# A two-layer S5 and linear-attention trunk: the first layer opens with all four u tiles accumulated together over k

## Chip, cores and metric

The kernel runs on 1 core of one Trainium2 chip. The metric is the time of one execution on the device in microseconds, as the median of several runs. A profile of one further execution is used to read where the time goes. TensorE is PE in the rows, VectorE DVE, ScalarE ACT, GpSimd POOL, and SP is the engine that issues the transfers.

## What is computed

The input x is 512 tokens of 1024 features. Each of two layers does this (cut from the reference, in float32):

```python
h = rmsnorm(x, norm_mix[i]);  z = h @ w_in[i]            # 1024 x 2064
u, q, k, v, g, gate_lr = split(z)                        # 512, 256, 256, 512, 512, 16 columns
y = s5(u)      # per channel group: complex diagonal recurrence of 64 states, y = Re(C s) + D u
y = gelu(y);  y = y * sigmoid(y @ w_glu + b_glu);  y_s5 = rmsnorm(y, s5_out_norm)
log_a = log_sigmoid(gate_lr @ w_gate + b_gate) / 16      # forget gate of the linear attention
cum = cumsum(log_a in chunks of 64);  q*exp(cum), k*exp(-cum), k*exp(last - cum)
o = causal(q k^T) v + q state;  y_gla = silu(g) * rmsnorm_per_head(o)
x = x + concat(y_s5, y_gla) @ w_out[i]
x = x + swiglu(rmsnorm(x, norm_ffn[i]))                  # 1024 -> 2 x 2816 -> 1024
```

A last RMS norm follows. The S5 part needs tables that depend on parameters alone: the step factor `a` of the recurrence, its powers `a1` to `a4`, the scaled input matrix `bb`, and rotation tables (cosine and sine per state and position).

## The kernel before

**Layout.** Activations are held transposed, features on the 128 partitions and 512 tokens along the free axis, as 8 tiles `xT[k]`. A weight block is 128x128, a weight unit 8 blocks (512 KB), in the order of the list that `block_order` returns. Every weight unit and every activation is split into a rounded half `hi` and a rest `lo`; a product is three matmuls (lines 576 to 578), so a dense tile of 8 k blocks has 24 of them. For a unit, ScalarE converts `hi` (L163) and VectorE subtracts for `lo` (L165). `Weights.ensure` keeps the splits `LOOK` units ahead; raw weights have 2 buffers and split ones 3, so a unit's load waits until the unit two before it is split.

**The RMS norm** is not applied to x. Its factor `rstd` is a row over tokens that scales the products afterwards: `R["rstd"]`. It comes from squares (ScalarE L598), their sum on POOL (L602), a matmul with ones and a logarithm and exponential on ScalarE (`norm`).

**The opening of a layer** is `u_pair`: u tiles 0 and 1 are accumulated together over k, then the 16 matmuls of the gate's low-rank input (`r_tile`, L756), then u tile 2, and inside it, after block k = 3, `stats`: the norm, the scaled row `rsb` (L706), the factor `rU` laid out in S5 order (four copies, L687) and u tile 0's evacuation. `u_copy` has ScalarE copy a u tile from PSUM in 16 pieces of 32x128 into S5 order (L745); `u_scale` then has VectorE multiply it by `rU`, from SBUF into SBUF (L738). `gate_a` does the gate product (L768, needs `rsb`), three passes on ScalarE (L772, L775, L776) and one on VectorE (L774); `gate_c` a subtraction, the cumulative sum and a subtraction on VectorE (L783 to L786); `gate_b` three exponentials (L795 to L797).

**Tables of layer 0** are made beside this in steps, which `bg0` deals out: `prep_small` (small VectorE operations, L304 and its neighbours: first the step, then `a1`, `fr` and `fi`, last `a2` to `a4`), `prep_w` (`bb` on VectorE, the sets with `a2` and `a3` on POOL, `a1` on VectorE, transposes L441 and transfers into `Wk`), `prep_v` (four sets on POOL) and `prep_rot` (rotation tables, on POOL L567 to L572). In layer 0 step 0 of `bg0` stands in `stats`, after `rU`, and makes `a2` to `a4` and `bb`.

**Order.** PE, ScalarE and SP run in the written order throughout; VectorE only in a region of layer 0 that begins at `u_pair` and ends ahead of `v_tiles`, and in the first FFN. Elsewhere VectorE's order, and POOL's everywhere, is set by a scheduler that plans with estimated times.

**Layer 0 after u:** q, k, q, k, then g 0 to 2, then `v_tiles`, whose 8 k steps have hooks for the S5 blocks b = 0 to 3: `s5_fwd` (8 matmuls, four VectorE multiplies L841 to L844 with the rotation tables, two POOL additions L846 and L847, eight scans L852), `s5_back` (four multiplies, POOL L869 and L874), `s5_y` (12 matmuls, 16 pieces of gelu on ScalarE, L899). `score` masks with L982. The GLU follows and needs all four y tiles.

Of the kernel before, what the change touches and what calls it, by code (L numbers as in the profile page):

```python
# [88 lines left out]

def block_order():  # L90
    order = [("in", k, n * P) for k in range(KD) for n in range(2)]
    for n in (2, 3):
        order += [("in", k, n * P) for k in range(KD)]
    for n in (0, 2, 1, 3):
        order += [("in", k, O_Q + n * P) for k in range(KD)]
    for n in range(3):
        order += [("in", k, O_G + n * P) for k in range(KD)]
    for k in range(KD):
        order += [("in", k, O_V + n * P) for n in range(4)]
    order += [("in", k, O_G + 3 * P) for k in range(KD)]  # L100
# [21 lines left out]
ORDER = block_order()  # L122
BIDX = {b: i for i, b in enumerate(ORDER)}
NUNIT = len(ORDER) // UB
assert NUNIT * UB == len(ORDER) == len(BIDX)


class Weights:
# [45 lines left out]
    def get(self, l, blk, width=1):  # L174
        b = BIDX[blk]
# [9 lines left out]
def tile_trunk(  # L185
# [49 lines left out]
    def startup():  # L235
# [411 lines left out]
    def mix(l, xp, nxt, bg):  # L647
# [33 lines left out]

        def unit_rows():
            rU = R["rU"] = act(f"rU{l}", F32, (P, P))
            rv = ntc(R["rstd"])
            for t in range(TS):
                h = slice(32 * t, 32 * t + 32)
                nc.vector.tensor_copy(rU[h].rearrange("p (n c) -> p n c", n=NCH), rv[h, :, t, :])  # L687

        U = {}
# [8 lines left out]
        def u_pair():  # L698
            ps = pair(lambda k: ("in", k, 0), lambda k: ("in", k, P), f"u{l}")
            r_tile()  # L700
            ssq = split(f"sqm{l}", xp.ss.acc) if l else xp.ss.acc

            def stats():
                norm(ssq)
                with tc.high_priority():
                    nc.vector.tensor_tensor(R["r"], R["psr"], R["rstd"], op=M)  # L706
                unit_rows()
                if l == 0:
                    bg()
                u_evac(0, ps[0])  # L710
                W.LOOK = 2

            if l == 0:
                W.LOOK = 1
# [7 lines left out]
            u_evac(2, ps2)  # L722

        def u_tile(b, mid=None):
            ps = dense(lambda k: ("in", k, b * P), f"u{l}{b}")
            if mid is not None:
                mid()
            u_copy(b, ps)
            if l == 0:
                bg()  # L730
            u_scale(b)

        def u_evac(b, ps):
            u_copy(b, ps)
            u_scale(b)

        def u_scale(b):
            nc.vector.tensor_tensor(U[b], U[b], bcast(R["rU"], [P, 4, P], 1), op=M)  # L738

        def u_copy(b, ps):  # L740
            u = act(f"U{l}{b}", F32, (P, 4, P))
            pv = ntc(ps)
# [6 lines left out]
            U[b] = u  # L749

        def r_tile():
            psr = R["psr"] = psum(f"r{l}")
            for k0 in (0, 4):
                for j in range(4):
                    k = k0 + j
                    nc.tensor.matmul(  # L756
                        psr[32 * j:32 * j + 32], wr_s[:, k], xT[k], start=(k0 == 0), stop=(k0 == 4),
                    )
# [278 lines left out]
        hg = cp.tile([P, 8], F32, tag="hg", name=f"hg{l}")  # L1037
        nc.vector.tensor_scalar(hbias, S(l, "bglu"), 0.5, None, op0=M)
        nc.vector.tensor_scalar(hg[:, 0:4], S(l, "s5n"), 0.5, None, op0=M)
        nsilu = 3 if l == 0 else 0  # L1040
        if nsilu:
            nc.vector.tensor_copy(hg[:, 4:4 + nsilu], S(l, "glan")[:, 0:nsilu])
        nc.vector.tensor_scalar(hg[:, 4 + nsilu:8], S(l, "glan")[:, nsilu:], 0.5, None, op0=M)
        ss = SumSq(f"s5{l}")
# [93 lines left out]
        else:  # L1138
            region.enter_context(tc.manual_schedule(engines={mybir.EngineType.DVE}))
            u_pair()  # L1140
            bg()
            bg()
            u_tile(3, lambda: (gate_b(0), gate_b(1)))
            q_tile(0)
            bg()
            k_tile(0)
            bg()
            q_tile(1)
            bg()
            k_tile(1)  # L1150
            bg()
            g_tile(0)
            bg()
# [5 lines left out]
            bg()  # L1159
            region.close()  # L1160
            v_tiles({
# [181 lines left out]
    with tc.manual_schedule(engines={mybir.EngineType.PE, mybir.EngineType.Activation, mybir.EngineType.SP}):  # L1343
        startup()
        xp = XPrep(0, "nmix")
# [6 lines left out]
        next(head)  # L1352
        for k in range(KD):
            xp.split(k)
            if k == 1:
                next(head)
            if k == 3:
                W.LOOK = 1
                W.ensure(0)
            if k > 2:  # L1360
                xp.ss.add(xT[k - 3])
        W.LOOK = 2
        next(small_)
        r_weights(0)
        W.ensure(0)
        for k in range(KD - 3, KD):
            xp.ss.add(xT[k])
        pl = prep_load(0, blks)
        nc.sync.dma_start(cst, const[:, 0:NCST])
        next(small_)  # L1370
        next(rots)
        nc.sync.dma_start(sml[1], small[1])
        pw_ = prep_w(0, nc.vector, pl)
        pv_ = prep_v(0, nc.gpsimd, pl)
        next(pv_)
        step0 = [0]
# [57 lines left out]
def lay_out(a):  # L1434
# [6 lines left out]
    for l in range(DEPTH):  # L1441
        for i, (m, k, c) in enumerate(ORDER):
            wst[l, i // UB, :, i % UB] = f[mats[m]][l, k * P:(k + 1) * P, c:c + P]
# [66 lines left out]
```

## Time and profile before

| | |
|---|---|
| median of 3 runs | 1159.95 us (1159.47 to 1160.25) |
| the profiled execution | 1159.86 us, its span 1158.1 us |
| TensorE busy | 1110.1 us, 96% of the span |
| VectorE busy | 706.2 us, 61% |
| ScalarE busy | 485.6 us, 42% |
| POOL busy | 331.9 us, 29% |
| HBM read | 100.52 MB |

The span is the stretch from the first to the last instruction of the profile. Busy time is summed over the whole span, and stages in it have different limits; the stretches say more. Matmul ends are modelled, and spans on POOL are rough. A group's name says what is written and read; Ln is line n of the kernel before.

### The profile page before, as it was taken

To read this page: it belongs to the slowest core of one execution; us is meant where nothing else is said; L and a number is where in the kernel's file an instruction comes from. 1 tells how busy PE (TensorE), PEld (TensorE's weight loads), DVE (VectorE), ACT (ScalarE), POOL (GpSimd) and SP (SyncE) were. 2 spreads that over 40 slices of the span, in tenths; PEclk is the share of its full clock that TensorE was granted. 3 is DMA by queue.
4 is the path that set the end of the run, shared out by engine and by line. 5 is a ranking of instruction groups with operands and counts; after the bars stand their busy time and mean duration, and the time that the engine had idled before them with its cause. 6 is when DMAs were issued, how large, how long until landed. Compare 5 with 4: busy or idle time off the path is not lost.

```text
span 1158.1 us, 13973 instructions
## 1 busy us (share of the span) xinstructions
PE 1110.1 (96%) x5316; PEld 913.9 (79%) x5316; DVE 706.2 (61%) x947; ACT 485.6 (42%) x844; POOL 331.9 (29%) x322
## 2 busy tenths in 40 slices
PE   8789779999999999999999799999999999999997
PEld 5568658888888888888887688888888888888886
DVE  7996976866454454564466994686545444444454
ACT  6853458443232232432358653745323222222243
POOL 6899544546000052065030440352000000000003
PEclk9899889999999999999999999999999999999999
DMA  6155111244343523232331212123332333223221
GB/s 211 55 112 126 37 37 37 92 130 116 103 109 100 137 91 101 82 109 91 93 104 41 73 61 85 56 91 94 107 100 85 106 99 102 91 91 109 91 91 73
DMA packets 64099, 107.72 MB, mean 93 GB/s; under 512 B 37408, under 2 KB 38304, under 8 KB 64032
## 3 DMA queue, kind: packets, MB, share of 16 engines
q1 hardware_dynamic: 63888, 106.56, 30.2%
q8 instruction: 42, 0.69, 0.2%
q10 hardware_dynamic: 144, 0.26, 0.1%
q14 instruction: 25, 0.20, 0.1%
HBM read 100.52 MB, written 2.10 MB: 89 GB/s over the span
## 4 chain that ended last, share of the span: by engine, by line
PE 79%; DVE 12%; ACT 3%; issue 2%; POOL 2%; DMA 1%; SPq 1%; DVEq 0%; POOLq 0%; ACTq 0%
PE fg L576 7%; PE fg L577 7%; PE fg L578 7%; PE fu L578 7%; PE fu L576 7%; PE fu L577 7%; PE fo L578 7%; PE fo L576 7%; PE fo L577 7%; DVE ro L852 2%; DVE wlo L165 2%; ACT U L745 1%; DVE qz L814 1%; DMA wrr<-in_wr_dram 1%; DMA raw<-in_wst_dram 1%
## 5 line engine op out<-in xcount | busy, mean ns | idle before, releaser
L165 DVE TENSOR_TENSOR wlo<-raw,whi 128x1024 fp32r<-128x1024 f32 x182 | 242.2, 1333 | 113.2 <-ACT whi L163 112.0
L163 ACT CAST whi<-raw 128x1024 fp32r<-128x1024 f32 x183 | 191.8, 1050 | 280.0 <-PE fo L577 116.9
L602 POOL TENSOR_TENSOR sq_fin<-sq_fin 128x512 f32<-128x512 f32 x5 | 6.5, 1296 | 341.8 <-ACT sq_fin L598 341.8
L1237 DVE TENSOR_TENSOR fu<-fu,rs_ffn 128x512 f32<-128x512 f32 x44 | 30.4, 691 | 116.7 <-PE fu L578 113.9
L1254 DVE TENSOR_TENSOR xall<-xall,fo 128x512 f32<-128x512 f32 x78 | 53.1, 686 | 61.9 <-PE fo L578 61.7
L1234 DVE TENSOR_TENSOR fg<-fg,rs_ffn 128x512 f32<-128x512 f32 x44 | 30.3, 688 | 34.7 <-PE fg L578 30.8
L1236 ACT ACTIVATE fg<-fg 128x512 f32<-128x512 f32 x44 | 27.7, 629 | 42.5 <-DVE fg L1234 42.4
L899 ACT ACTIVATE y<-y 32x128 f32<-32x128 f32 x128 | 34.4, 269 | 20.9 <-PE y L890 17.3
L1238 DVE TENSOR_TENSOR fu<-fg,fu 128x512 f32<-128x512 f32 x44 | 31.3, 711 | 5.7 <-ACT fg L1236 1.3
L745 ACT COPY U<-u 32x128 f32<-32x128 f32 x128 | 32.9, 257 | 1.5
L852 DVE TENSOR_TENSOR_SCAN ro<-sp_mag,ro 128x128 f32<-128x128 f32 x64 | 28.5, 507 | 6.6 <-POOL ro L846 6.6
L1089 POOL TENSOR_TENSOR xall<-xall,wo 128x512 f32<-128x512 f32 x16 | 25.5, 1613 | 24.0 <-DVE wo L1088 24.0
L407 POOL TENSOR_TENSOR pt<-bc,sp_a1r 128x256 f32<-128x256 f32 x2 | 1.7, 852 | 94.0 <-issue 92.0
L568 POOL TENSOR_TENSOR rt<-rg 128x512 f32<-128x512 f32 x8 | 10.2, 1288 | 59.8 <-ACT rg L548 59.7
L602 POOL TENSOR_TENSOR sq_s<-sq_s,sq_s 128x512 f32<-128x512 f32 x6 | 8.1, 1342 | 64.3 <-ACT sq_s L598 64.3
L869 POOL TENSOR_TENSOR sr<-ro,ro 128x508 f32<-128x508 f32 x8 | 14.6, 1826 | 39.3 <-DVE ro L867 39.3
L602 POOL TENSOR_TENSOR sq_x1nmix<-sq_x1nmix 128x512 f32<-128x512 f32 x7 | 9.2, 1315 | 57.3 <-ACT sq_x1nmix L598 57.3
L890 PE MATMUL y<-sr,Vx 128*128 128x128 f32 x64 | 15.0, 322 | 8.0 <-POOL sr L869 7.8
L890 PE MATMUL y<-sm,Vx 128*128 128x128 f32 x64 | 14.8, 318 | 6.2 <-POOL sm L874 6.2
L888 PE MATMUL y<-U,Tz 128*128 128x128 f32 x64 | 14.9, 320 | 5.5 <-DVE ro L842 5.4
L846 POOL TENSOR_TENSOR ro<-ro,ro 128x512 f32<-128x512 f32 x8 | 10.7, 1344 | 30.8 <-DVE ro L843 30.8
L890 PEld LDWEIGHTS y<-sr,Vx 128*128 128x128 f32 x64 | 11.9, 231 | 8.9 <-POOL sr L869 8.9
(1257 smaller groups left out, 3533.0 us busy)
## 6 DMA issues: line engine op xcount, KB each, us to landing
raw<-in_wst_dram SPq DMA_DIRECT2D x183, 512.0 KB, 3.5
Wk<-wt SPq DMA_DIRECT2D x64, 64.0 KB, 3.9
xall<-in_xt_dram SPq DMA_DIRECT2D x3, 512.0 KB, 8.5
out_dram<-fin SPq DMA_DIRECT2D x6, 256.0 KB, 2.2
bc<-in_s5bc_dram SPq DMA_DIRECT2D x4, 256.0 KB, 4.1
raw<-in_wst_dram SPq DMA_DIRECT2D x1, 384.0 KB, 5.8
cst<-in_const_dram SPq DMA_DIRECT2D x1, 384.0 KB, 5.0
xall<-in_xt_dram SPq DMA_DIRECT2D x1, 283.0 KB, 3.0
```

Of the source, the lines that this page charges most:

```text
L163: self.nc.scalar.copy(hi, raw)
L165: (self.nc.gpsimd if v in POOL_W else self.nc.vector).tensor_tensor(lo, raw, hi.bitcast(F32), op=ALU.subtract)
L576: nc.tensor.matmul(ps, whi, xh, start=start, stop=False)
L577: nc.tensor.matmul(ps, whi, xl, start=False, stop=False)
L578: nc.tensor.matmul(ps, wlo, xh, start=False, stop=stop)
L745: nc.scalar.copy(u[32 * t:32 * t + 32, j].rearrange("p (n c) -> p n c", n=NCH), pv[32 * j:32 * j + 32, :, t, :],)
L852: v.tensor_tensor_scan(dst[:, cs], sp["mag4"][:, c:c + 1].to_broadcast([P, P]), src[:, cs], 0.0, M, A)
L890: nc.tensor.matmul(o, Vx[:, pr, part, 1:].rearrange("p a b c -> p (a b c)"), s_[:, cs], start=False, stop=(part == 1),)
L899: nc.scalar.activation(yv[32 * j:32 * j + 32, :, t, :], ps[32 * t:32 * t + 32, j * P:(j + 1) * P].rearrange("p (n c) -> p n c", n=NCH), AF ...
L1237: nc.vector.tensor_tensor(u, pu, rstd[0], op=M)
L1238: nc.vector.tensor_tensor(u, g, u, op=M)
L1254: nc.vector.tensor_tensor(xT[n], xT[n], ps[n], op=A)
```

## The change

Layer 0 gets its own block order. All four u tiles are accumulated together (`u_quad`): for each k the products of the four, with the first new `bg` step after k = 2 and, after k = 6, the gate's row products, the norm and `rsb`; then k = 7. The gate product follows at once, then g0, q0, k0, q1, k1, g1, g2. Scaling and copying change places in both layers: VectorE multiplies the u tile by `rstd` while it reads PSUM, into a new tile `us`, and ScalarE copies that from SBUF into S5 order. `rU` is gone. The tile of the row products moves to the other PSUM pool tag.

The first weight loads are split 4 and 4 blocks instead of 2 and 6, x comes in 8 transfers instead of 5, and x6 and x7 are issued behind the load of unit 2. VectorE's written order now begins at the start of the kernel. `prep_small`'s first part stands ahead of x6; `r_weights`, the table loads, the second part and the rotation arguments move into the step `rest` after k = 2 (step -1 of `bg0`). Step 0, with `a2` to `a4` and `bb`, stands after `gate_c` and the first u copy. Four small gain operations move from the start to the end of the region (in layer 1 to the GLU).

```diff
-def block_order():
-    order = [("in", k, n * P) for k in range(KD) for n in range(2)]
-    for n in (2, 3):
-        order += [("in", k, n * P) for k in range(KD)]
+def block_order(l):
+    wide = 2 if l else 4
+    order = [("in", k, n * P) for k in range(KD) for n in range(wide)]
+    for n in range(wide, 4):
+        order += col(n * P)
+    if l == 0:
+        order += col(O_G)
     for n in (0, 2, 1, 3):
-        order += [("in", k, O_Q + n * P) for k in range(KD)]
-    for n in range(3):
-        order += [("in", k, O_G + n * P) for k in range(KD)]
+        order += col(O_Q + n * P)
+    for n in range(0 if l else 1, 3):
+        order += col(O_G + n * P)
...
-        for a, b in ((0, 2), (2, 8)):
+        for a, b in ((0, 4), (4, 8)):
...
-        load_w(0, 2)
+        load_w(0, 4)
         load_x(1, 2)
-        load_w(2, 8)
-        load_x(2, 4)
+        load_w(4, 8)
+        load_x(2, 3)
         W.load(1)
-        load_x(4, 6)
-        load_x(6, 8)
+        load_x(3, 4)
         nc.sync.dma_start(lam, s5l)
+        load_x(4, 5)
+        load_x(5, 6)
         wr_load(0)
+        yield
+        load_x(6, 7)
+        load_x(7, 8)
...
-            ps2 = dense(lambda k: ("in", k, 2 * P), f"u{l}2", at={NORM_AT: stats})
+            ssq = split(f"sqm{l}", xp.ss.acc)
+            ps2 = dense(lambda k: ("in", k, 2 * P), f"u{l}2", at={NORM_AT: lambda: (norm(ssq), rows(), u_evac(0, ps[0]))})
             gate_a(0)
             gate_a(1)
-            u_copy(1, ps[1])
+            u_scale(1, ps[1])
+            u_copy(1)
             gate_c(0)
             gate_c(1)
-            u_scale(1)
             u_evac(2, ps2)
+
+        def u_quad():
+            ps = [psum(f"u{l}{n}") for n in range(4)]
+            for k in range(KD):
+                for n in range(4):
+                    hi, lo = W.get(l, ("in", k, n * P))
+                    mm3(ps[n], hi, lo, xp.h[k], xp.l[k], k == 0, k == KD - 1)
+                if k == 2:
+                    bg()
+                if k == KD - 2:
+                    r_tile()
+                    norm(xp.ss.acc)
+                    rows()
+            return ps
...
-        def u_scale(b):
-            nc.vector.tensor_tensor(U[b], U[b], bcast(R["rU"], [P, 4, P], 1), op=M)
+        def u_scale(b, ps):
+            t = us[b] = act(f"us{l}{b}")
+            nc.vector.tensor_tensor(t, ps, R["rstd"], op=M)
...
-            region.enter_context(tc.manual_schedule(engines={mybir.EngineType.DVE}))
-            u_pair()
+            ups_ = u_quad()
+            u_scale(0, ups_[0])
+            gate_a(0)
+            gate_a(1)
+            for n in (1, 2, 3):
+                u_scale(n, ups_[n])
+            W.ensure(4)
+            gate_c(0)
+            gate_c(1)
+            u_copy(0)
+            bg()
+            gate_b(0)
+            gate_b(1)
+            g_tile(0)
             bg()
             bg()
-            u_tile(3, lambda: (gate_b(0), gate_b(1)))
+            u_copy(1)
+            bg()
             q_tile(0)
+            u_copy(2)
             bg()
             k_tile(0)
             bg()
             q_tile(1)
             bg()
+            u_copy(3)
             k_tile(1)
             bg()
-            g_tile(0)
             bg()
             g_tile(1)
...
+        xp.split(0)
+        next(head)
+        xp.split(1)
+        xp.split(2)
+        W.LOOK = 1
+        W.ensure(0)
+        next(loads, None)
+        xp.split(3)
+        xp.ss.add(xT[0])
+        xp.ss.add(xT[1])
+        xp.split(4)
+        xp.ss.add(xT[2])
         W.LOOK = 2
+        W.ensure(0)
+        xp.split(5)
+        xp.ss.add(xT[3])
         next(small_)
...
+        def rest():
+            r_weights(0)
+            pl = prep_load(0, blks)
+            nc.sync.dma_start(cst, const[:, 0:NCST])
+            next(small_)
+            next(rots)
+            nc.sync.dma_start(sml[1], small[1])
+            gens["w"] = prep_w(0, nc.vector, pl)
+            gens["v"] = prep_v(0, nc.gpsimd, pl)
+            next(gens["v"])
```

## Rows read from the trace of the kernel before

**Rows 1.** from:to, length; busy of PE, PEld, DVE, ACT, POOL; clock, DMA, GB/s.

```profile
0.00:171.00 171.00, 139.03 (x735) 108.90 (x735) 147.07 (x241) 100.86 (x231) 129.48 (x136) 0.94 0.36 98
...
640.00:680.00 40.00, 32.44 (x177) 27.93 (x176) 39.87 (x67) 21.85 (x58) 19.96 (x20) 0.96 0.18 56
```

**Rows 2.** TensorE in order of time, layer 0 (start, length, in brackets idle before).

```profile
36.74 3.78 PE L768 MATMUL gt<-rsb,sml 128*128 128x512 f32 x4 [5.15 <-DVE rsb L706]
...
124.07 0.76 PE L888 MATMUL y<-U,Tz 128*128 128x128 f32 x2 [5.38 <-DVE ro L842]
...
170.22 0.50 PE L576 MATMUL gl<-yg03h,whi 128*128 128x512 f32 x1 [3.04 <-ACT yg03h L583]
```

**Rows 3.** POOL in order of time, layer 0.

```profile
38.41 0.62 POOL L407 TENSOR_TENSOR pt<-bc,sp_a2r 128x256 f32<-128x256 f32 x1 [1.95 <-DVE sp_a2i L304]
...
46.26 3.54 POOL L407 TENSOR_TENSOR pt<-bb,sp_a2r 128x256 f32<-128x256 f32 x1 [2.33 <-DVE bb L412]
...
51.51 1.07 POOL L407 TENSOR_TENSOR pt<-bb,sp_a3r 128x256 f32<-128x256 f32 x1
...
56.08 0.98 POOL L462 MEMSET wk<- 128x512 f32 x2
...
77.94 1.34 POOL L813 MEMSET qz<- 64x256 f32 x4
...
112.49 1.29 POOL L846 TENSOR_TENSOR ro<-ro,ro 128x512 f32<-128x512 f32 x1
...
126.66 1.26 POOL L846 TENSOR_TENSOR ro<-ro,ro 128x512 f32<-128x512 f32 x1
...
137.48 1.26 POOL L846 TENSOR_TENSOR ro<-ro,ro 128x512 f32<-128x512 f32 x1
```

**Rows 4.** VectorE in order of time, layer 0.

```profile
36.06 0.62 DVE L706 TENSOR_TENSOR rsb<-r,rs_mix 128x512 f32<-128x512 f32 x1
...
38.52 0.55 DVE L304 TENSOR_TENSOR sp_a2i<-sp_a2i,sptmp 128x32 f32<-128x32 f32 x1
...
46.96 2.35 DVE L165 TENSOR_TENSOR wlo<-raw,whi 128x1024 fp32r<-128x1024 f32 x2
...
113.81 4.54 DVE L852 TENSOR_TENSOR_SCAN ro<-sp_mag,ro 128x128 f32<-128x128 f32 x4 [4.61 <-POOL ro L846]
...
122.63 0.69 DVE L841 TENSOR_TENSOR ro<-x,cosT 128x512 f32<-128x512 f32 x1
...
126.61 1.81 DVE L982 COPY_PREDICATED sc<-cst,sc 64x256 f32<-64x256 uint32 x4
```

**Rows 5.** ScalarE in order of time, layer 0.

```profile
39.39 1.05 ACT L163 CAST whi<-raw 128x1024 fp32r<-128x1024 f32 x1 [3.31 <-DMA raw<-in_wst_dram]
40.46 1.18 ACT L772 ACTIVATE ab<-gt,xall 128x512 f32<-128x512 f32 x1
...
44.82 0.72 ACT L776 ACTIVATE ab<-ab,bias 128x512 f32<-128x512 f32 x1
```

**Rows 6.** groups by line and shape (busy us, mean ns of one).

```profile
L745 ACT COPY U<-u 32x128 f32<-32x128 f32 x128 | 32.9, 257 | 1.5
...
L524 ACT COPY Tz<-Tz 32x128 f32<-32x128 f32 x8 | 2.4, 296 | 0.1
...
L738 DVE TENSOR_TENSOR U<-U,rU 128x512 f32<-128x512 f32 x8 | 7.1, 903 | 4.5 <-ACT U L745 4.3
```

**Rows 7.** VectorE in order of time, opening of layer 1.

```profile
615.14 0.90 DVE L687 COPY rU<-rs_mix 32x128 f32<-32x128 f32 x4
...
626.75 0.68 DVE L783 TENSOR_TENSOR mn<-mn,ab 128x512 f32<-128x512 f32 x1
...
628.72 0.69 DVE L786 TENSOR_TENSOR mn<-ab 128x512 f32<-128x512 f32 x1
...
639.00 0.17 DVE L799 COPY dec<-E 128x8 f32<-128x8 f32 x1 [1.31 <-ACT E L795]
```

**Rows 8.** TensorE in order of time, opening of layer 1.

```profile
646.38 0.49 PE L890 MATMUL y<-sr,Vx 128*128 128x128 f32 x2 [2.28 <-POOL sr L869]
```

More of the change, by code (lines that the diff above doesn't have):

```diff
@@ L87, with col @@
 TAIL = [("glu", n) for n in range(4)] + [("s5", n) for n in range(KD)] + [("gla", n) for n in range(KD)]
-def block_order():
-    order = [("in", k, n * P) for k in range(KD) for n in range(2)]
-    for n in (2, 3):
-        order += [("in", k, n * P) for k in range(KD)]
+def block_order(l):
+    def col(n):
+        return [("in", k, n) for k in range(KD)]
+    wide = 2 if l else 4
[4 more added lines that the diff above has]
+        order += col(O_G)
     for n in (0, 2, 1, 3):
-        order += [("in", k, O_Q + n * P) for k in range(KD)]
-    for n in range(3):
-        order += [("in", k, O_G + n * P) for k in range(KD)]
+        order += col(O_Q + n * P)
+    for n in range(0 if l else 1, 3):
+        order += col(O_G + n * P)
     for k in range(KD):
         order += [("in", k, O_V + n * P) for n in range(4)]
-    order += [("in", k, O_G + 3 * P) for k in range(KD)]
+    order += col(O_G + 3 * P)
     for what, n in TAIL:
@@ L119, in block_order @@
     return order
[L122 to L125, printed above, removed]
+ORDER = [block_order(l) for l in range(DEPTH)]
+BIDX = [{b: i for i, b in enumerate(o)} for o in ORDER]
+NUNIT = len(ORDER[0]) // UB
+assert all(NUNIT * UB == len(o) == len(b) for o, b in zip(ORDER, BIDX))
 class Weights:
@@ L174, in get @@
     def get(self, l, blk, width=1):
-        b = BIDX[blk]
+        b = BIDX[l][blk]
         u = l * NUNIT + b // UB
@@ L680, in norm @@
             nc.scalar.activation(rcol, rcol, AF.Exp, scale=-1.0)
[L682 to L687, printed above, removed]
         U = {}
@@ L700, in u_pair, with rows @@
             r_tile()
[L701 to L714, printed above, removed]
-            ps2 = dense(lambda k: ("in", k, 2 * P), f"u{l}2", at={NORM_AT: stats})
+            ssq = split(f"sqm{l}", xp.ss.acc)
+            ps2 = dense(lambda k: ("in", k, 2 * P), f"u{l}2", at={NORM_AT: lambda: (norm(ssq), rows(), u_evac(0, ps[0]))})
             gate_a(0)
             gate_a(1)
-            u_copy(1, ps[1])
+            u_scale(1, ps[1])
+            u_copy(1)
             gate_c(0)
             gate_c(1)
-            u_scale(1)
             u_evac(2, ps2)
+        def u_quad():
[11 more added lines that the diff above has]
+            return ps
+        def rows():
+            with tc.high_priority():
+                nc.vector.tensor_tensor(R["r"], R["psr"], R["rstd"], op=M)
         def u_tile(b, mid=None):
@@ L727, in u_tile, with u_copy @@
                 mid()
[L728 to L731, printed above, removed]
+            u_evac(b, ps)
         def u_evac(b, ps):
[L734 to L742 removed]
+            u_scale(b, ps)
+            u_copy(b)
+        us = {}
+        def u_scale(b, ps):
+            t = us[b] = act(f"us{l}{b}")
+            nc.vector.tensor_tensor(t, ps, R["rstd"], op=M)
+        def u_copy(b):
+            u = U[b] = act(f"U{l}{b}", F32, (P, 4, P))
+            pv = ntc(us.pop(b))
             for j in range(4):
@@ L756, in r_tile @@
                     nc.tensor.matmul(
-                        psr[32 * j:32 * j + 32], wr_s[:, k], xT[k], start=(k0 == 0), stop=(k0 == 4),
+                        psr[32 * j:32 * j + 32], wrs[l][:, k], xT[k], start=(k0 == 0), stop=(k0 == 4),
                     )
@@ L1037, in mix, with gains @@
         hg = cp.tile([P, 8], F32, tag="hg", name=f"hg{l}")
-        nc.vector.tensor_scalar(hbias, S(l, "bglu"), 0.5, None, op0=M)
-        nc.vector.tensor_scalar(hg[:, 0:4], S(l, "s5n"), 0.5, None, op0=M)
         nsilu = 3 if l == 0 else 0
-        if nsilu:
-            nc.vector.tensor_copy(hg[:, 4:4 + nsilu], S(l, "glan")[:, 0:nsilu])
-        nc.vector.tensor_scalar(hg[:, 4 + nsilu:8], S(l, "glan")[:, nsilu:], 0.5, None, op0=M)
+        def gains():
+            nc.vector.tensor_scalar(hbias, S(l, "bglu"), 0.5, None, op0=M)
+            nc.vector.tensor_scalar(hg[:, 0:4], S(l, "s5n"), 0.5, None, op0=M)
+            if nsilu:
+                nc.vector.tensor_copy(hg[:, 4:4 + nsilu], S(l, "glan")[:, 0:nsilu])
+            nc.vector.tensor_scalar(hg[:, 4 + nsilu:8], S(l, "glan")[:, nsilu:], 0.5, None, op0=M)
         ss = SumSq(f"s5{l}")
@@ L1159, in mix @@
             bg()
-            region.close()
+            gains()
+            dve0.close()
             v_tiles({
@@ L1195, in mix @@
         })
+        if l > 0:
+            gains()
         for key in TAIL:
@@ L1343, in tile_trunk @@
     with tc.manual_schedule(engines={mybir.EngineType.PE, mybir.EngineType.Activation, mybir.EngineType.SP}):
-        startup()
+        dve0 = ExitStack()
+        dve0.enter_context(tc.manual_schedule(engines={mybir.EngineType.DVE}))
+        loads = startup()
+        next(loads)
+        constants()
         xp = XPrep(0, "nmix")
@@ L1352, in tile_trunk @@
         next(head)
[L1353 to L1361, printed above, removed]
+        xp.split(0)
[10 more added lines that the diff above has]
+        xp.ss.add(xT[2])
         W.LOOK = 2
+        W.ensure(0)
+        xp.split(5)
+        xp.ss.add(xT[3])
         next(small_)
[L1364 to L1376, printed above, removed]
+        xp.split(6)
+        xp.ss.add(xT[4])
+        xp.ss.add(xT[5])
+        xp.split(7)
+        xp.ss.add(xT[6])
+        xp.ss.add(xT[7])
+        def rest():
[8 more added lines that the diff above has]
+            next(gens["v"])
+        gens = {}
+        step0 = [-1]
         BG_W = (1, 0, 2, 1, 1, 1, 1, 1, 1, 1)
@@ L1382, in bg0 @@
             step0[0] += 1
+            if i < 0:
+                rest()
+                return
+            pw_, pv_ = gens["w"], gens["v"]
             if i == 0:
@@ L1441, in lay_out @@
     for l in range(DEPTH):
-        for i, (m, k, c) in enumerate(ORDER):
+        for i, (m, k, c) in enumerate(ORDER[l]):
             wst[l, i // UB, :, i % UB] = f[mats[m]][l, k * P:(k + 1) * P, c:c + P]
```

6 lines of the change are left out of this document (2 added, 4 removed).

## The prediction, as put on record

> **What bounds the kernel now.** I read the stretches first. TensorE is busy for 1110.1 of 1158.1 us, so it idles 48. Of these, 171 - 139.03 = 32 lie before 171 us and 40 - 32.44 = 7.6 between 640 and 680 [rows 1]. So two places can give or lose time: the first layer up to its GLU, and the opening of the second layer. Every microsecond by which either shifts is passed on whole, since TensorE has no slack behind them.
>
> Next, what ends TensorE's waits in the first layer [rows 2]. The gate product waits 5.15 us for the scaled row `rsb`, the first S5 output tile 5.38 us, and the stage ends when the last S5 tile has passed ScalarE (170.22). The dense products themselves wait little. The S5 chain begins when POOL adds the first rotated block (L846 at 112.49).
>
> What holds that addition is POOL's own queue [rows 3]. POOL gets the second complex power at 38.41, waits 2.33 us for `bb`, starts the third set of products at 46.26, and works from there to 112.49 without a wait. So the first layer's end hangs on when POOL can start at `a2` and how fast it goes, and only then on TensorE. This is the reading on which I forecast: the change works on the TensorE and VectorE front, and POOL's start is a by-product.
>
> **The change part by part.** All times below are from the profiled execution, 1159.86 us with a span of 1158.1; the median of the runs is 1159.95, which is the same for this purpose.
>
> *Quad and loads.* Four u tiles over k need units 0 to 3 instead of 0 and 1 while x arrives. TensorE's work is the same and only moved forward. The extra cost is on VectorE: two more weight subtractions stand ahead of `rsb`, 2 x 1.18 = 2.35 us [rows 4]. Against that, the squares now end sooner, since five of the sums stand before the last x parts. I take +1 us on `rsb`, so 37 instead of 36.06; ends -2.5 (all hidden in VectorE's early gaps) and +2.5. TensorE's wait for `rsb` shrinks, because row sums and u3 are now in front of it. That saves TensorE up to the 5.15 us of that wait [rows 2], but it only arrives earlier at the S5 wait, so I count nothing. The second x pair waiting behind one weight load on the SP queue, and the gains moved behind, cost nothing as long as L846 is late; without that cover it is the 1 to 2 us by which x6 may come late.
>
> *a2 moves behind the gates.* In the old order VectorE went from `rsb` almost straight to the powers: `a2i` done at 38.52 + 0.55 = 39.07 [rows 4]. In the new order the gate block stands between. From `rsb` at 37.0 + 0.6: the first gate product takes at most half the 3.78 us of the pair [rows 2]. That pair ran right after the 5.15 us wait, which is shorter now, so I take 1.0, until 38.6 (at worst 0.9 more). Then ScalarE's two gate chains, 40.46 to 45.54 = 5.1 us, and the conversion of unit 6 behind them, 1.05 [rows 5], and its subtraction, 1.2: 45.9. The three u scalings fit into that wait. The two cumulative sums without POOL beside them take 626.75 to 629.41 = 2.66 each in layer 1 [rows 7]: 51.2. The six small operations to `a2i` took 1.5 us for eight: about 1. So `a2` at 52.2 instead of 39.1: **+13 us** for POOL's start.
>
> *What POOL wins back.* (1) Before, the gate block, two weight subtractions and a U multiply ran beside POOL's third set. L407 took 3.54 us instead of 0.62, the next four products 51.51 to 56.08 = 4.6 instead of 2.5 [rows 3]: 5.0 us that no longer occur, since that work now lies before `a2`, while POOL waits. (2) The memsets that stand in POOL's busy stretch (0.98, and twice 1.34 [rows 3]) can be placed in the new wait: 0 to 3.7, I take 1.8. (3) The four U multiplies from SBUF become products read from PSUM; they took 0.90 us on average [rows 6] and three of them ran in POOL's stretch after the gates: 0 to 2.7, I take 1.0. (4) VectorE gets through its own list sooner (it is ahead by the dense work already done), so POOL's last tables see a quieter VectorE: 0 to 3, I take 2. Sum: 13 - 5.0 - 1.8 - 1.0 - 2 = **+3.2 us** for L846; ends -2 and +9.
>
> Behind point (3) stands a rule of the Trainium skill, SBUF — State Buffer, section "SBUF: two separate sides": a VectorE operation with two SBUF inputs and a GpSimd operation that reads SBUF hold the shared ports in turn, each for its whole instruction. The 3.54 us row agrees. By the rule in full point (3) would be worth 2.7 instead of 1.0, and the total 1.7 us less.
>
> *What VectorE wins behind L846.* With L846 held up and VectorE early, work that now sits between the first and second S5 block can be done before it: the second block's four multiplies with a weight subtraction and a small add (122.63 to 126.6) and the masked scores, 1.81 us [rows 4]. The first L846 to the second takes 14.2 us, the second to the third 10.8 [rows 3]. If the first gap becomes like the others: **-3.4 us**; ends 0 and -5.8. First layer together: -0.2.
>
> *Second layer.* The four rU copies go, 0.90 us [rows 7], and the U multiply becomes a product from PSUM: at the 0.62 us of `rsb`, which reads PSUM too [rows 4], 4 x (0.90 - 0.62) = 1.1. VectorE is busy 39.87 of 40 us there [rows 1], so up to -2.0. Against it: ScalarE's copies begin only after `rsb` and the first scaling (+1.2), and they read SBUF. A 32x128 copy out of SBUF took 296 ns, out of PSUM 257 [rows 6]: 16 x 0.039 = 0.6 per tile, three tiles ahead of the gate exponentials, which VectorE waits for once (1.31 us [rows 7]): up to +3.0. But the waits of TensorE there end on POOL's S5 rows [rows 8], which follow VectorE. I take **-0.6**, ends -2.0 and +3.0.
>
> A rule of the Trainium skill speaks against the change here: VectorE: DVE Perf Modes, section "The TRN2 errata", gives ScalarE 224 cycles ahead of the elements for SBUF to SBUF and 172 from PSUM, at 1.2 GHz 43 ns more per copy, an estimate from that page. The 39 ns of the rows agree. By the page the three tiles cost 2.1 us instead of 1.9; what is open is only whether ScalarE's chain is the late one.
>
> Sum: +3.2 - 3.4 - 0.6 = -0.8, so **1159 us**: the front gets faster and the S5 chain does not start earlier for it.
>
> **Rivals.** *Faster, about 1152.* POOL catches up: memsets all inside the wait, VectorE out of its way, so L846 comes 2 us earlier (110.5), and the second S5 block is fully prepared (-5.8), layer 2 as forecast. 1159.9 - 2 - 5.8 - 0.6 = 1151.5. For it: one product stretched from 0.62 to 3.54 shows how much of POOL's 74 us from 38.41 to 112.49 can be waiting inside instructions [rows 3]. Against: POOL shows no wait after 46.26, so each gain has to come out of such instructions.
>
> *Slower, about 1167.* The powers behind the gates cost POOL its start and nothing makes it up: 13 - 5.0 = +8 on L846, VectorE's order behind it stays as it is, -0.6: 1167.3. Place: POOL's wait ahead of the first product with `a2`. It decides from the point where L846 starts after about 118. For it: only the 5.0 us are sure to go, the rest is POOL's order, which the scheduler chooses. Against: VectorE already waited for POOL in front of the first scans, which with 4.54 us for four show POOL beside them [rows 4].
>
> *ScalarE sets layer 2, about 1163.* First layer as forecast, second +3.0: 1162.7. For it: the 1.31 us wait; against: rows 8.
>
> *The quad stalls, about 1162.* The subtraction of unit 3 stands behind the small S5 operations and x7. If `rsb` comes at 40 instead of 37, all of the chain to `a2` moves by 3: 1162. A sign that the change doesn't do what it says would be that TensorE waits inside the quad for several microseconds.
>
> **How the numbers follow.** This kernel's timing can tell 0.2%, 2.3 us, from no change. Forecast, near 1159 with its own range 1155 to 1163: 0.46, of which 0.16 faster, 0.24 the same, 0.06 slower. Faster rival: 0.24. Slower rival: 0.20. The two smaller ones, 1162 to 1163: 0.10, of which 0.03 count as the same. That gives faster 0.40, same 0.27, slower 0.33. The range for 8 in 10 takes in both large rivals up to their middle: 1150 to 1167.
>
> **What would show it.** Right: `rsb` near 37; POOL waiting from about 35 to 52 and then none until L846 at 114 to 118; TensorE idle at the first S5 output for longer than 5.4 us, with v products ahead of it done by about 105; L846 to the second L846 near 11 us; no rU copies; U copies near 0.30 us. Wrong: L846 before 110 or after 120; POOL idle in its stretch; the second layer's idle 7.6 us changed by more than 2; or a stage behind 171 us that isn't dense.

## The result and the profile after

The changed kernel takes 1168.36 us (median of 4 runs, 1166.54 to 1169.04), the kernel before 1159.71 beside it (1159.43 to 1160.25): a ratio of 1.0072 with a 95% interval of 1.0054 to 1.0089. That is 8.7 us slower, where 1159 with a range of 1150 to 1167 was forecast. The profiled execution took 1166.54 us (span 1164.8), the fastest of the four; it lies 6.7 over that of before, so about 2 us of the loss in the medians are not in this profile.

The stretches first (columns as in [rows 1]), each moved by the 6 us by which the end of the first layer's S5 part has moved:

```profile
0.00:177.00 177.00, 140.32 (x735) 111.84 (x735) 142.20 (x237) 103.07 (x231) 118.99 (x136) 0.90 0.34 94
646.00:686.00 40.00, 33.26 (x176) 28.65 (x175) 38.40 (x69) 25.59 (x62) 20.09 (x20) 0.91 0.21 66
```

TensorE idles 177 - 140.32 = 36.7 us in the first and 6.7 in the second, against 32.0 and 7.6 [rows 1]. Most of the loss is in the first layer. Not all of it is idle time: over the whole span TensorE idles 52.0 us for 48.0, and is busy 2.7 us longer with the same products, at a mean granted clock of 0.979 for 0.987. TensorE's longest waits in the changed kernel, answering [rows 2, 8]:

```profile
26.80 0.80 PE L590 MATMUL u<-x6h,wlo 128*128 128x512 f32 x1 [2.31 <-DVE wlo L171]
...
39.15 1.98 PE L775 MATMUL gt<-rsb,sml 128*128 128x512 f32 x4 [1.75 <-DVE rsb L730]
...
63.52 0.80 PE L590 MATMUL q<-x0h,wlo 128*128 128x512 f32 x1 [4.47 <-DVE wlo L171]
...
77.54 0.79 PE L590 MATMUL k<-x0h,wlo 128*128 128x512 f32 x1 [4.63 <-DVE wlo L171]
...
132.31 0.76 PE L895 MATMUL y<-U,Tz 128*128 128x128 f32 x2 [5.66 <-DVE ro L849]
...
176.25 0.50 PE L588 MATMUL gl<-yg03h,whi 128*128 128x512 f32 x1 [3.02 <-ACT yg03h L595]
...
655.62 0.80 PE L897 MATMUL y<-sr,Vx 128*128 128x128 f32 x2 [4.65 <-POOL sr L876]
```

The wait for `rsb` has shrunk from 5.15 to 1.75. What the quad won there, TensorE loses again: 2.31 inside the quad, 4.47 at q1 and 4.63 at k1, each for a weight half, and the first S5 output still waits 5.66. The stage ends at 176.25 instead of 170.22: +6.0. POOL, answering [rows 3]:

```profile
53.72 0.62 POOL L419 TENSOR_TENSOR pt<-bc,sp_a2r 128x256 f32<-128x256 f32 x1 [16.31 <-DVE sp_a2i L316]
...
61.53 0.70 POOL L419 TENSOR_TENSOR pt<-bb,sp_a2r 128x256 f32<-128x256 f32 x1 [2.32 <-DVE bb L424]
...
67.38 0.98 POOL L474 MEMSET wk<- 128x512 f32 x2
...
78.49 1.33 POOL L820 MEMSET qz<- 64x256 f32 x4
...
118.95 1.28 POOL L853 TENSOR_TENSOR ro<-ro,ro 128x512 f32<-128x512 f32 x1
...
133.19 1.27 POOL L853 TENSOR_TENSOR ro<-ro,ro 128x512 f32<-128x512 f32 x1
...
144.01 1.27 POOL L853 TENSOR_TENSOR ro<-ro,ro 128x512 f32<-128x512 f32 x1
```

POOL stands still for 16.31 us ahead of `a2`, starts it 15.3 later than before and has made up 8.9 of that when the first addition starts (L853, which was L846): 118.95, +6.5. About 1.1 of the 8.9 is one product (`rt<-rk,rg`) that stood ahead of the addition before and that the scheduler has now put behind it, so that POOL does 73 operations up to there instead of 74. From there the gaps are the old ones, 14.2 and 10.8. VectorE, answering [rows 4]:

```profile
35.05 3.44 DVE L171 TENSOR_TENSOR wlo<-raw,whi 128x1024 fp32r<-128x1024 f32 x2
38.41 0.68 DVE L730 TENSOR_TENSOR rsb<-r,rs_mix 128x512 f32<-128x512 f32 x1
...
53.84 0.55 DVE L316 TENSOR_TENSOR sp_a2i<-sp_a2i,sptmp 128x32 f32<-128x32 f32 x1
...
71.09 0.61 DVE L421 TENSOR_TENSOR pt<-bb,sp_a1i 128x256 f32<-128x256 f32 x1 [3.04 <-ACT U L753]
...
120.26 3.98 DVE L859 TENSOR_TENSOR_SCAN ro<-sp_mag,ro 128x128 f32<-128x128 f32 x3 [3.07 <-POOL ro L853]
...
130.88 0.69 DVE L848 TENSOR_TENSOR ro<-x,cosT 128x512 f32<-128x512 f32 x1
```

`rsb` is at 38.41 behind two subtractions that took 3.44 us; `a2i` is done at 54.4. At 71.09 VectorE waits 3.04 us in `prep_w`'s product for ScalarE's copy of a u tile, a wait that the kernel before does not have. In front of the first scans it idles 3.07, and the second block's multiplies begin at 130.88. In the second layer, answering [rows 7]:

```profile
648.25 0.17 DVE L806 COPY dec<-E 128x8 f32<-128x8 f32 x1 [1.48 <-ACT E L802]
```

E's last column is read 9.3 us later, 3.3 more than the shift of the first layer.

To compare kernels I use the last pass of the GLU with the last S5 tile (its start is the last number ahead of the semicolon) as the end of each layer's S5 part. Before, first and second layer:

```profile
L578 PE MATMUL gl<-yg03h,wlo x4: 393/393/632, 171.4 to 187.3; 128*128 128x512 f32 x4
...
L578 PE MATMUL gl<-yg13h,wlo x4: 387/391/393, 724.7 to 739.2; 128*128 128x512 f32 x4
```

After, first and second layer:

```profile
L590 PE MATMUL gl<-yg03h,wlo x4: 389/393/628, 177.6 to 193.2; 128*128 128x512 f32 x4
...
L590 PE MATMUL gl<-yg13h,wlo x4: 387/391/393, 731.7 to 746.1; 128*128 128x512 f32 x4
```

187.3 has become 193.2 (+5.9). From the first layer's mark to the second's it was 739.2 - 187.3 = 551.9 and is 746.1 - 193.2 = 552.9 (+1.0). What follows is 0.2 shorter. Together +6.7.

### The profile page after: what moved, and what is told of

Same layout as the page of the kernel before. It is cut to its first block, busy times and chain, and to the rows that moved or that the text cites. A ratio compares the mean times of both kernels' runs of the same rounds, so it can differ in the third digit from the quotient of the medians.

```text
span 1164.8 us, 13974 instructions
## 1 busy us (share of the span) xinstructions
PE 1112.8 (96%) x5316; PEld 917.9 (79%) x5316; DVE 697.5 (60%) x939; ACT 490.6 (42%) x844; POOL 321.3 (28%) x322
## 4 chain that ended last, share of the span: by engine, by line
PE 80%; DVE 8%; POOL 6%; ACT 4%; issue 2%; DMA 1%; SPq 0%; DVEq 0%; POOLq 0%; ACTq 0%
PE fg L588 7%; PE fg L589 7%; PE fu L589 7%; PE fg L590 7%; PE fu L588 7%; PE fu L590 7%; PE fo L588 7%; PE fo L590 7%; PE fo L589 7%; DVE ro L859 1%; ACT U L753 1%; DVE wlo L171 1%; DMA raw<-in_wst_dram 1%; ACT y L906 1%; PE v L920 1%
## 5 line engine op out<-in xcount | busy, mean ns | idle before, releaser
L171 DVE TENSOR_TENSOR wlo<-raw,whi 128x1024 fp32r<-128x1024 f32 x182 | 244.7, 1348 | 126.4 <-ACT whi L169 125.1
L753 ACT COPY U<-us 32x128 f32<-32x128 f32 x128 | 37.9, 296 | 6.5 <-DVE wk L424 2.3
L840 PE MATMUL x<-U,Wk 128*128 128x128 f32 x128 | 17.2, 288 | 4.6 <-DMA Wk<-wt 4.3
L840 PEld LDWEIGHTS x<-U,Wk 128*128 128x128 f32 x128 | 16.3, 202 | 5.6 <-ACT whi L169 2.8
L897 PE MATMUL y<-sm,Vx 128*128 128x128 f32 x64 | 15.3, 327 | 4.3 <-POOL sm L881 4.3
```

The lines of the kernel that those rows point to most:

```text
L171: (self.nc.gpsimd if v in POOL_W else self.nc.vector).tensor_tensor(lo, raw, hi.bitcast(F32), op=ALU.subtract)
L753: nc.scalar.copy(u[32 * t:32 * t + 32, j].rearrange("p (n c) -> p n c", n=NCH), pv[32 * j:32 * j + 32, :, t, :],)
L840: nc.tensor.matmul(ps[part][:, j * P:(j + 1) * P], Wk[:, part, 4 * b + j], U[b][:, j], start=True, stop=True,)
L897: nc.tensor.matmul(o, Vx[:, pr, part, 1:].rearrange("p a b c -> p (a b c)"), s_[:, cs], start=False, stop=(part == 1),)
```

## Experiments

All kernels in one table, from their profiled executions and the medians; the kernel before had a median of 1159.95 to 1160.10 beside them.

| kernel | POOL starts `a2` | first addition | end of S5, layer 0 | from there to layer 1's | median us |
|---|---|---|---|---|---|
| before | 38.41 | 112.49 | 187.3 | 551.9 | 1159.95 |
| after | 53.72 | 118.95 | 193.2 | 552.9 | 1168.36 |
| 1 powers early | 41.31 | 117.31 | 190.1 | 552.9 | 1164.25 |
| 2 before, powers late | 50.65 | 117.61 | 192.9 | 551.9 | 1165.74 |
| 3 before, scaled from PSUM | 37.19 | 123.85 | 197.7 | 554.3 | 1172.30 |
| 4 after, layer 1 scaled as before | 53.75 | 119.0 | 192.9 | 551.9 | 1165.25 |
| 5 after, `us` elsewhere | 53.77 | 118.39 | 192.7 | 554.6 | 1168.10 |
| 6 = 1 + 5 | 40.07 | 112.48 | 185.6 | 554.3 | 1160.78 |
| 7 = 1 + 5 + 4 | 40.70 | 113.16 | 188.4 | 552.0 | 1160.41 |
| 8 after, block 1 early | 54.14 | 119.2 | 195.9 | 553.0 | 1170.06 |
| 9 = 7 + 8 | 40.06 | 112.49 | 190.0 | 552.3 | 1162.77 |
| 10 = 7, scales first | 41.60 | 112.15 | 187.2 | 552.3 | 1159.96 |

**1. Powers early.** One part of the change undone.

```diff
             u_scale(0, ups_[0])
+            bg()
             gate_a(0)
...
             u_copy(0)
-            bg()
             gate_b(0)
```

> One part of the change undone: in the changed kernel, background step 0 (powers a2 to a4, a2i and their products) is issued on VectorE right behind the first scaled u tile, ahead of the gate products, instead of behind both gate blocks. POOL's own order is the changed kernel's. Theory 1 (the late start of POOL costs the time): POOL's first product with a2 starts near 41 us instead of 53.72, the first addition of the rotated pair at or before 113 us instead of 118.95, the end of layer 0's gl near 171 instead of 176.25, and the time is about 1161 to 1163, 5 to 7 us under the changed kernel's 1168.4. Rival A (ScalarE's copies of the scaled tiles and TensorE's stalls between 58 and 78 us cost it): POOL starts early but waits later, the addition stays above 116 us and the time at 1166 to 1169. Rival B (the gates, now 8 us later, become the bound): POOL is early, E and the q tiles late, time 1163 to 1168.

1164.25 us, ratio 1.0037 [1.0024, 1.0049]: 4.1 us of the loss come back, a time between theory 1 and rival A, with rival A's late wait. It also lies in rival B's range (the gates as the bound); experiment 6 speaks against that, since it is 3.5 us faster although the second gate's E begins at 59.4 us there, nearly as late as here (60.6; 54.2 in the changed kernel). POOL in time:

```profile
41.31 0.62 POOL L419 TENSOR_TENSOR pt<-bc,sp_a2r 128x256 f32<-128x256 f32 x1 [4.85 <-DVE sp_a2i L316]
...
74.75 0.66 POOL L421 TENSOR_TENSOR pt<-bc,sp_a3i 128x256 f32<-128x256 f32 x1 [7.97 <-DVE pt L422]
...
117.31 1.30 POOL L853 TENSOR_TENSOR ro<-ro,ro 128x512 f32<-128x512 f32 x1
```

POOL starts 12.4 us earlier and then stops for 7.97 us in the middle of a product. What VectorE waits for at that time:

```profile
73.84 0.43 DVE L421 TENSOR_TENSOR pt<-bb,sp_a1i 128x256 f32<-128x256 f32 x1 [3.29 <-ACT U L753]
```

So the late start is one cause, and something else takes its place as soon as it is gone. As I read it, VectorE's product needs a buffer that a u tile holds until ScalarE has copied it (the 45 shared ones go round in turn), and POOL's product stands behind VectorE's; experiments 5 and 6 test that.

**2. Only late.** The kernel before with the one move alone.

```diff
                 unit_rows()
-                if l == 0:
-                    bg()
...
             gate_c(1)
+            if l == 0:
+                bg()
             u_scale(1)
```

> The kernel before with one thing of the change alone: background step 0 is issued behind the gates' scans instead of inside the third u tile. Theory 1: POOL's first product with a2 comes 8 to 14 us later than 38.41, the first addition of the rotated pair 4 to 8 us later than 112.49, and the time is 4 to 7 us above 1159.9. Rival A (copies and stalls of the new u tiles are the cause, a late start is made up by POOL): the addition at 112 to 114, time 1159 to 1161.

1165.74 us, 1.0048 [1.0035, 1.0060], +5.7, as theory 1 says:

```profile
50.65 0.63 POOL L407 TENSOR_TENSOR pt<-bc,sp_a2r 128x256 f32<-128x256 f32 x1 [14.52 <-DVE sp_a2i L304]
...
117.61 1.30 POOL L846 TENSOR_TENSOR ro<-ro,ro 128x512 f32<-128x512 f32 x1
```

Start +12.2, first addition +5.1, end of the stage +5.7. (Two of the products `rt<-rk,rg` have moved behind the addition here.) The late powers alone make two thirds of the loss, without quad, loads or scaling.

**3. Scaling alone**, in the order of before.

```diff
-        def u_scale(b):
-            nc.vector.tensor_tensor(U[b], U[b], bcast(R["rU"], [P, 4, P], 1), op=M)
+        def u_scale(b, ps):
+            t = us[b] = act(f"us{l}{b}")
+            nc.vector.tensor_tensor(t, ps, R["rstd"], op=M)
```

> The kernel before with the u tiles scaled on VectorE as PSUM is read, and then copied from SBUF by ScalarE, in both layers; order of tiles and gates as before. Theory 2 (the scaled-first order puts ScalarE's slower SBUF copies behind VectorE and costs about 3 us where the second layer's E waits for ScalarE): E's last column is read near 642 instead of 639, time 1 to 3 us above before. Rival: four VectorE copies of the row scale and the slower multiplications saved, 1 to 2 us faster than before.

1172.30 us, 1.0103 [1.0088, 1.0119]: +12.3, four times what the theory gave, and of it 10.4 in the first layer, which neither reading had. The waits of VectorE (total, times, longest) and then POOL:

```profile
DVE wlo L165 <- ACT whi L163: 8.9, 3, 6.0
DVE wt L441 <- ACT bk L436: 6.2, 1, 6.2
```

```profile
37.19 0.62 POOL L407 TENSOR_TENSOR pt<-bc,sp_a2r 128x256 f32<-128x256 f32 x1 [1.02 <-DVE sp_a2i L304]
...
76.49 0.62 POOL L409 TENSOR_TENSOR pt<-bc,sp_a3i 128x256 f32<-128x256 f32 x1 [15.30 <-DMA Wk<-wt]
...
123.85 1.30 POOL L846 TENSOR_TENSOR ro<-ro,ro 128x512 f32<-128x512 f32 x1
```

ScalarE's copy of u0 now waits for VectorE, which is busy with the powers, and everything behind it on ScalarE waits too: weight halves (VectorE stands 6.0 for one) and the copies of `bb` (6.2). POOL stands 15.30 us in the middle of a product, until a transfer of the transposed `bb` copies is through. A part of the change alone is thus worse than the whole. As I read it, the new order of the first layer, with the first scaling ahead of the powers, is what made the scaling bearable; no run changes that alone.

**4. Old scaling in the second layer** of the changed kernel.

```diff
-            u_scale(b, ps)
-            u_copy(b)
+            u_copy(b, ps)
+            u_late(b)
```

> The changed kernel with the second layer's scaling as it was before (ScalarE copies PSUM, VectorE multiplies the copy by the rearranged row scale); the first layer as changed. Theory 2: E's last column in the second layer comes about 3 us earlier against the layer's start, time 0.7 to 3 us under the changed kernel's 1168.4. Rival (the second layer has slack there): no difference, 1167.5 to 1169.

1165.25 us, 1.0046 [1.0033, 1.0059], 3.1 under the changed kernel by the medians and 1.3 from profile to profile, so the rival falls. The last column of E:

```profile
644.63 0.17 DVE L816 COPY dec<-E 128x8 f32<-128x8 f32 x1 [1.31 <-ACT E L812]
```

That is 451.7 us behind the first layer's mark, as before (639.0 - 187.3); with the new scaling it was 455.0 (after, experiment 1) to 455.5 (experiment 5). The stretch between the marks is 551.9 again. In this kernel both kinds of copy stand side by side (busy us, mean ns; answers [rows 6]):

```profile
L763 ACT COPY U<-us 32x128 f32<-32x128 f32 x64 | 18.9, 296 | 4.5 <-DVE wk L424 2.3 <-DVE wt L453 1.5
L763 ACT COPY U<-u 32x128 f32<-32x128 f32 x64 | 16.4, 256 | 0.8
```

**5. The scaled tiles elsewhere.** They go to the first halves of the rotation tables, which are empty until POOL writes them.

```diff
-            t = us[b] = act(f"us{l}{b}")
+            if l == 0:
+                t = (cosT, sinT)[b % 2][:, 4 * (b // 2):4 * (b // 2) + 4].rearrange("p a b -> p (a b)")
...
+            us[b] = t
```

> The changed kernel, with the first layer's four scaled u tiles put into the still empty first halves of the rotation tables (cosT, sinT) instead of four of the 45 shared buffers. Everything else as changed. Theory 3 (in the changed kernel POOL is set by its late start alone, the buffers cost VectorE 3.0 us at its product pt but not the end): VectorE's 3.04 us wait for ScalarE's copy goes, POOL's first addition of the rotated pair stays between 117.5 and 119, the time between 1166.5 and 1168.5. Rival (the buffers are what keeps VectorE from getting ahead, and with it cost the time): the addition below 117, time 1163 to 1166.

1168.10 us, 1.0070 [1.0056, 1.0084]: no difference, as theory 3 says. VectorE's 3.04 us wait is gone (the product runs at 68.04 without one), but POOL reaches the first addition hardly earlier:

```profile
53.77 0.63 POOL L419 TENSOR_TENSOR pt<-bc,sp_a2r 128x256 f32<-128x256 f32 x1 [16.60 <-DVE sp_a2i L316]
...
118.39 1.29 POOL L857 TENSOR_TENSOR ro<-ro,ro 128x512 f32<-128x512 f32 x1
```

**6. Both**, 1 and 5 together.

> Powers early (step 0 right behind the first scaled u tile) and the scaled u tiles in the rotation tables as well. Theory 3 (with the powers early, POOL's 8.0 us wait in the middle is a wait for one of the 45 shared buffers, which the scaled tiles hold until ScalarE has copied them): that wait falls to under 2 us, POOL's first addition of the rotated pair comes at 109 to 113 instead of 117.3, and the time is 1159 to 1161.5, 3 to 5 us under the kernel with the powers early alone (1164.3). Rival A (VectorE's own lateness in its product holds POOL, not a buffer): the wait stays at 4 us or more, time 1163 to 1165. Rival B (the addition comes early but the second block's inputs are late): addition under 113, time 1162 to 1164.

1160.78 us (11 runs), 1.0010 [1.0001, 1.0019], 3.5 under experiment 1 and 7.6 under the changed kernel:

```profile
40.07 0.62 POOL L419 TENSOR_TENSOR pt<-bc,sp_a2r 128x256 f32<-128x256 f32 x1 [3.99 <-DVE sp_a2i L316]
...
63.02 0.62 POOL L421 TENSOR_TENSOR pt<-bc,sp_a3i 128x256 f32<-128x256 f32 x1
...
69.79 1.35 POOL L824 MEMSET qz<- 64x256 f32 x4 [3.09 <-DVE pt L422]
...
112.48 1.28 POOL L857 TENSOR_TENSOR ro<-ro,ro 128x512 f32<-128x512 f32 x1 [0.36 <-DVE ro L854]
```

The product that had waited 7.97 us runs at 63.02 without a wait; 3.09 are left at a memset behind it. The first addition is at 112.48, where it was before the change. Two causes stood in series: the buffer alone is worth 0.3 us (5), which is within the noise, the order alone 4.1 (1), both 7.6. That the addition comes at the very time of before is partly chance: against before, POOL starts at `a2` 1.7 later, waits 5.4 longer and spends 7.1 less in its instructions (1.1 of it the moved product), and at the end it waits 0.36 for VectorE.

**7. All three**, 4 added.

> Powers early, scaled u tiles of the first layer in the rotation tables, and the second layer scaled as before the change. Theory: the three effects add up: first layer as with the former two, the second layer back by 2 to 3 us, time 1156 to 1159, at or under the kernel before (1160.0). Rival (the second layer's gain was a matter of how the first ended): 1159 to 1161.5, no better than with the first two.

1160.41 us (11 runs), 1.0004 [0.9995, 1.0013]. The stretch between the marks falls by 2.3, but the median only by 0.4: the rival's range. What ate it in the profile lies in the first layer, whose instructions stand in the same order in 6 and 7 (last section).

**8 and 9. The second S5 block early**, to get the 3.4 us that the prediction had counted on; 8 from the changed kernel, 9 from experiment 7.

```diff
-                2: [lambda: s5_back(0), bg],
-                3: [lambda: s5_fwd(1)],
+                2: [lambda: s5_fwd(1), lambda: s5_back(0), bg],
```

> The changed kernel with the second S5 block's input (TensorE's x products and VectorE's four multiplies with the rotation tables) issued one v stage earlier, ahead of the first block's way back. Theory 4 (the gain of 3.4 us that the prediction expected behind POOL's first addition failed because the second block's x products stand so late in TensorE's order, at 118.0, that VectorE idles 3.07 us in front of the first scans): VectorE's idle time there falls under 1 us, the end of layer 0 comes 2 to 3.5 us earlier than in the changed kernel, time 1165 to 1166.5. Rival (POOL's remaining table work or the PSUM buffers bind there, not the order): end of layer 0 unchanged within 1 us, time 1167.5 to 1169.

> The three repairs (powers early, scaled tiles of the first layer in the rotation tables, second layer scaled as before) with the second S5 block's input one v stage earlier as well. Theory 4: with the tables done at 113 VectorE still has 1 to 2 us of idle time in front of the first scans to fill; time 1157.5 to 1159.5, under the kernel before (1160.0) by 0.5 to 2.5. Rival: the chain of the four blocks is VectorE's work and nothing is idle in it, time 1160 to 1161.5.

1170.06 us, 1.0089 [1.0075, 1.0102], and 1162.77, 1.0029 [1.0017, 1.0040]: both slower, theory 4 and rival missed. The scans of the first three blocks in experiment 8 and, below, of the second and third in the changed kernel:

```profile
120.55 5.36 DVE L859 TENSOR_TENSOR_SCAN ro<-sp_mag,ro 128x128 f32<-128x128 f32 x4 [0.38 <-POOL ro L853]
...
134.24 3.63 DVE L859 TENSOR_TENSOR_SCAN ro<-sp_mag,ro 128x128 f32<-128x128 f32 x8
...
146.71 2.43 DVE L859 TENSOR_TENSOR_SCAN ro<-sp_mag,ro 128x128 f32<-128x128 f32 x4 [0.87 <-POOL ro L853]
```

```profile
136.69 2.62 DVE L859 TENSOR_TENSOR_SCAN ro<-sp_mag,ro 128x128 f32<-128x128 f32 x8
...
145.31 2.42 DVE L859 TENSOR_TENSOR_SCAN ro<-sp_mag,ro 128x128 f32<-128x128 f32 x4 [1.10 <-POOL ro L853]
```

The idle time went (0.38 instead of 3.07), as theory 4 says, and the second block's scans came 2.45 us earlier. The third block's came 1.4 later. Its x products on TensorE stand behind the first block's output, which now comes later, and behind a PSUM buffer that the masked scores free; in experiment 8 and, below, in the changed kernel:

```profile
143.39 1.13 PE L840 MATMUL x<-U,Wk 128*128 128x128 f32 x8 [2.58 <-DVE sc L989]
```

```profile
136.81 1.95 PE L840 MATMUL x<-U,Wk 128*128 128x128 f32 x16
```

**10. All scales first**: experiment 7 with the four `u_scale` ahead of the powers.

> The three repairs, with all four u tiles scaled ahead of the powers instead of the first alone. Theory (TensorE's q product waits 2.6 to 4.4 us for a PSUM buffer that VectorE frees only behind the powers, and that costs time): that wait goes, POOL starts a2 2 us later; time 1158 to 1160. Rival (POOL's start is what counts, TensorE's wait is absorbed at the S5 output): first addition 1.5 to 2.5 us later than 113.2, time 1161 to 1163.

1159.96 us (11 runs), 1.0000 [0.9992, 1.0009]. TensorE's wait at q0 went, as the theory says (4.36 in 7), but one of 4.37 for a weight half stands at q1 instead. POOL starts 0.9 us later than in 7 and the first addition is at 112.15, so the rival falls. Its median is the lowest of the repaired kernels, though 0.4 under experiment 7 is within the noise, and equals the one before; none beats it.

## Why the prediction was wrong

**The reading held, the forecast did not.** The first layer's end hangs on when POOL starts at `a2` and how fast it goes. Experiment 2 moves that start alone and gets +5.7 us. Experiments 6, 7 and 10, which have the quad, the loads, the gate order and the new scaling (7 and 10 in the first layer only), but POOL's first addition at 112.2 to 113.2, take as long as the kernel before within 0.1%. So the front's gain came to nothing in every kernel tried.

**The step that failed: "What VectorE wins behind L846", -3.4, was 0.** The first gap was 14.24 us, as before. VectorE was not early: its last table transpose began at 96.13 instead of 95.29. As I read it, the quad's lead was spent on the waits shown above: TensorE's at q1 and k1 for weight halves and VectorE's for a u copy. But that alone does not explain the gap: in experiment 5, without the u copy's wait, that transpose began at 94.01, and the gap was 14.4 us. The written order does: with the second block's x products and multiplies ahead of the first block's way back (experiment 8) the gap fell to 5.0. The end did not follow, since the gap behind it grew to 21.2: the third addition came 26.2 us after the first instead of 25.1. So the gap between the first two additions is not the quantity that the end follows; the third block waited for TensorE's written order. Of the signs that the prediction set for being right, the gap near 11 us and the addition at 114 to 118 did not come.

**L846: +3.2 forecast, +6.5 measured.** `rsb` was 1.4 later than taken (38.41 for 37; the two subtractions took 3.44 for 2.35). So it ended 1.5 late, at 39.09. From there to the end of `a2i` the sum had 14.6 us (37.6 to 52.2) and it took 15.3 (to 54.39), 0.7 more. So +15.3 instead of +13. Of the 9.8 that POOL was to win back it won 8.9. The stretch beside the gates (46.26 to 56.08 [rows 3], now 61.53 to 67.38) gave 4.0 for 5.0. The memsets did not move into the wait, as 67.38 and 78.49 show, so point (2) gave nothing. The rest of the stretch up to the addition gave 4.9, where points (2) to (4) have 4.8; that is partly luck, since about 1.1 of it is the product that moved behind the addition, which the sum did not have.

Point (3) by itself can be read: the multiply from PSUM takes 0.68 us for 0.90. The Trainium skill, SBUF — State Buffer, section "SBUF: two separate sides", had it that two-input SBUF work on VectorE and POOL's reads exclude one another; POOL's product with `a2` out of `bb` took 0.70 us at 61.53, with VectorE at small work, and 3.54 before beside a multiply of U and two weight subtractions [rows 3, 4], which agrees.

**Not seen at all: the buffers.** The change adds a tile per u block in the shared pool and holds it until ScalarE is through. The diff showed it, and I asked of every engine but not of the pool what comes free when. In the changed kernel it is covered by the late powers (experiment 5); with those gone it costs 3.5 us (6 against 1).

**Second layer: -0.6 forecast, +1.0 in the profiled execution.** The rival "ScalarE sets layer 2" had the mechanism and, for E, the size: +3.3 us for +3.0. Of that, 3 x 16 x 39 ns = 1.9 are the slower copies (296 against 256 to 257 ns); the rest I put down to the later start. TensorE's first wait there grew from 2.28 to 4.65, but its wait at the next block shrank from 3.32 to 0.79. So the +1.0 is not idle time: TensorE idles 6.7 us for 7.6 in the stretch of [rows 1], and the granted clock is 0.91 for 0.96. VectorE's saving was real, but it saves on an engine that waits for ScalarE at that place. The Trainium skill, VectorE: DVE Perf Modes, section "The TRN2 errata", gave an estimate of 43 ns per copy; the trace has 39. How much reaches the second mark varies: +1.0 to +1.1 in three profiles (after, 1, 8), +2.4 to +2.7 in three others (3, 5, 6). TensorE's wait at the first block is 4.6 us in all six, and at the next 0.6 to 1.1. What differs is the granted clock in the 10 us around that second wait, 1.00 in the former three and 0.83 in the latter. The changed kernel and, below, experiment 5 (length, busy, granted clock, DMA share, GB/s):

```profile
670.00:680.00 10.00, 9.26 (x60) 1.00 0.30 105
```

```profile
670.00:680.00 10.00, 9.26 (x53) 0.83 0.33 105
```

Why it falls in one kernel and not in the other is not shown.

**The slower rival**, 1167.3 with a chance of 0.20, came true within 1.1 us and through its own condition: the addition after 118. Its +8 on the addition was too much (6.5), its -0.6 for the second layer too little, so that it came so close is partly luck.

## What to carry to other kernels

When a change reorders the front, follow the first product that the slowest chain needs, here six small operations, and keep it where it was; a lead on engines that are not late is spent before it arrives. A new intermediate tile also takes a buffer for as long as its last reader takes, so ask of a shared pool what of an engine is asked: what stands behind it. Undo parts in pairs, since with two causes in series undoing one shows little (0.3 and 4.1 us, but 7.6 for both).

## What the hardware showed that was not expected

Experiments 6 and 7 have the same instructions in the same order in the first layer, yet its mark was at 185.6 in one profile and 188.4 in the other. TensorE around the wait for the last S5 tile, in 6 and then in 7 (length, busy, granted clock, DMA share, GB/s):

```profile
165.00:170.00 5.00, 3.40 (x29) 0.91 0.37 134
170.00:175.00 5.00, 4.67 (x42) 1.00 0.00 0
```

```profile
165.00:170.00 5.00, 1.20 (x6) 0.93 0.50 176
170.00:175.00 5.00, 4.21 (x9) 0.50 0.00 0
```

In 7 TensorE was busy for 1.20 of the 5 us up to 170 and came back at half the clock (0.50, the 1.2 GHz level); in 6 it was busy for 3.40 and came back at full clock (2.4 GHz). All marks of the first layer carry this. From TensorE's first pass with the last S5 tile to its last it took 15.5 us in experiments 1 and 6 (granted 1.00), 16.6 to 17.1 in before, after and experiments 2 to 5, 8 and 9 (0.91 in before and after), and 17.6 in 7 and 10 (0.83). A difference of 1 to 2 us between two kernels with such a wait needs more than one profile.
